# Trunk layer on one core: modulation sums of the first two k-tiles in one PSUM bank, squares of x added in pairs, and a new table for the background sums

## The chip, the cores and the metric

One NeuronCore of a Trainium2 chip runs the whole program. The metric is the device time of one execution in microseconds. Every span and duration below is from the hardware profiler.

## The reference, cut to what matters

One layer over 512 tokens of width 2048. All modulation vectors are columns of one product of a single row, silu(c), with the 2048 x 12288 matrix ada_w. The first normalisation and the modulation make h, and h goes through the input projection w_in:

```python
cond = jax.nn.silu(c)
mod = cond @ ada_w[l] + ada_b[l]
sh_m, sc_m, gt_m, sh_f, sc_f, gt_f = jnp.split(mod[:, None, :], 6, axis=-1)
h = rms_norm(x, mix_pre_g[l]) * (1.0 + sc_m) + sh_m
y = token_mixers(h, w_in[l], ...)
x = x + gt_m * rms_norm(y, mix_post_g[l])
h = rms_norm(x, ffn_pre_g[l]) * (1.0 + sc_f) + sh_f
y = conv_glu_ffn(h, ffn_w_up[l], ffn_conv_w[l], ffn_conv_b[l], ffn_w_down[l])
x = x + gt_f * rms_norm(y, ffn_post_g[l])
```

## The kernel before, in words

**Layout.** x is held transposed as 16 k-tiles of 128 channels x 512 tokens. An fp32 product is made of three matmuls on parts (`mm3`, L379 to L382): L380 is hi x hi of weight and h, L382 the weight's remainder `lo`, L381 the remainder `hl` of h. `split` (L364) makes the weight's parts: ScalarE copies `hi` (L373, L376) and, in the shadow form, a second copy `sh` to PSUM (L372); VectorE subtracts to give `lo` (L374, L377). `make_h` (L486) makes `hh` (L490) and the modulated tile (L491) on ScalarE and `hl` (L493) on VectorE for k-tile 0, on GpSimd for the others; `xn` (L495) multiplies x by the norm in the same way (L497).

**Order of the projection.** The columns of w_in that are taken first run in six steps over k (KSTEPS): four steps of two k-tiles (0, 1), (2, 3), (4, 5), (6, 7), and two of four. In each step five groups of columns (nine in the later steps) are multiplied into PSUM banks, and each result is added to a partial sum in SBUF: in step 0 by a copy on ScalarE (L604, L616), later by an addition on VectorE (L606, L618).

**Modulation columns.** h of a k-tile needs its modulation columns. A set `c` of columns (two k-tiles) is made of eight units and a closing entry (`mod_units`, L518). A unit (`gemv_unit`, L410) loads 256 rows of ada_w (512 KB, L415) into one of five `ada` buffers (NADA) and multiplies them by cond: units alternate between GpSimd (ScalarE scales, L430 and L434; GpSimd adds, L435) and VectorE (one instruction for scale and add, L428 and L432). The closing entry joins the two running sums on VectorE (`join`, L439), sums over partitions on TensorE by matmuls with a column of ones (L446), finishes the columns on VectorE (L450 to L452) and makes h of both k-tiles. For k-tiles 0 and 1 a unit is split in halves of 256 KB (L418), each k-tile's half having its own PSUM bank (`first_half`, L500); there units 1 and 4 go to GpSimd (HV), the others to VectorE, and the column sums are L510, L513 and L514.

**The start.** `x_norm` (L461) squares the 16 tiles of x on ScalarE (L471); of every four squares the first two are added on VectorE (L476), and the three results are summed by fp32 matmuls with a matrix of ones (L477), 12 in all; then come the square root (L478) and the reciprocal (L479).

**What sets the order.** All these loads are issued by SyncE's one queue, in the program's order; an issue waits where its buffer is still in use, and all behind it wait with it. The instructions of each engine are placed by a list scheduler, which goes by costs of its own. In the loop over KSTEPS (L656) closing and other entries of the sets are issued behind the groups: FS0 gives the numbers behind the groups of step 0, and in step s > 0 `upto` takes just the sets that step s + 1 needs, spread over the groups but the last two. This makes 9, 9, 9, 18 and 18 entries in steps 0 to 4.

Of the kernel before, what the change touches and what calls it, by code (L numbers as in the profile page):

```python
# [12 lines left out]
AF = mybir.ActivationFunctionType  # L13
ALU = mybir.AluOpType
# [6 lines left out]
KT = D // P  # L21
# [16 lines left out]
KSTEPS = [(0, 1), (2, 3), (4, 5), (6, 7), (8, 9, 10, 11), (12, 13, 14, 15)]  # L38
# [211 lines left out]
def trunk_kernel(ctx: ExitStack, tc: tile.TileContext, a: dict, out: bass.AP):  # L250
# [30 lines left out]
    def mt(s="m", shape=(P, 512), dt=F32):  # L281
        return cur[0].tile(list(shape), dt, tag="m", name=nm(s))
# [16 lines left out]
    def mx(s="mx"):  # L299
        return pp.tile([P, 512], F32, tag=mtag(), name=nm(s), bufs=2)  # L300
# [110 lines left out]
    def gemv_unit(accs, eng, uidx, i, half=None, bank=None):  # L411
        w = 512 if half is None else 256
        if half is None:
            raw = araw()
            nc.sync.dma_start(out=raw, in_=a["ada"][uidx])  # L415
        else:
            raw = mt("ada")
            nc.sync.dma_start(out=v2(raw), in_=v2(a["ada"][uidx])[:, :, half * 256:(half + 1) * 256])  # L418
        for j in range(2):
            c1 = cond[:, 2 * i + j:2 * i + j + 1]  # L420
            src = raw[:, j * w:(j + 1) * w]
            if eng not in accs:
                if eng is V and bank is not None:
                    accs[eng] = bank[:, :w]
                else:
                    accs[eng] = galloc("ga")[:, :w]
                if eng is V:
                    V.tensor_scalar(accs[eng], src, c1, None, ALU.mult)  # L428
                else:
                    S.activation(accs[eng], src, AF.Copy, scale=c1)  # L430
            elif eng is V:
                V.scalar_tensor_tensor(accs[eng], src, c1, accs[eng], ALU.mult, ALU.add)  # L432
            else:
                S.activation(src, src, AF.Copy, scale=c1)  # L434
                G.tensor_tensor(accs[eng], accs[eng], src, ALU.add)  # L435

    def join(accs):
        if len(accs) == 2:
            V.tensor_tensor(accs[G], accs[G], accs[V], ALU.add)  # L439
        return accs[G]  # L440
# [12 lines left out]
        return ca, cb  # L453


    xT = []
    for kt in range(KT):
        xT.append(hp.tile([P, 512], F32, tag=f"hl{kt}", name=nm("x")))
# [2 lines left out]
    def x_norm():  # L461

        ss = gp.tile([P, 512], F32, name="rB")
        warm = st(1)
        S.activation(warm, tc0[:, 0:1], AF.Square)
        S.activation(warm, warm, AF.Sqrt)
        ps = mx("xss")
        odd = None
        for kt in range(KT):
            sq = mt("sq")  # L470
            S.activation(sq, xT[kt], AF.Square)  # L471
            if kt % 4 == 0:
                odd = sq
                continue
            if kt % 4 == 1:
                V.tensor_tensor(sq, odd, sq, ALU.add)  # L476
            TE.matmul(ps, ones, sq, start=kt == 1, stop=kt == KT - 1)  # L477
        S.activation(ss, ps, AF.Sqrt, bias=epst, scale=1.0 / D)  # L478
        V.reciprocal(ss, ss)  # L479
        return ss  # L480

    rB = x_norm()

    hh, hl = [None] * KT, [None] * KT

# [11 lines left out]
        (G if kt else V).tensor_tensor(h_, xT[kt], rB, ALU.mult)  # L497
        return h_

    def first_half(kt):  # L500

        accs = {}
        bk = mx("ga")
        for i in range(8):
            gemv_unit(accs, (G if i in HV else V), gada[0][i], i, kt, bk)
        h_ = xn(kt)
        ga = join(accs)
        ps = bk[:, 256:258]
        for j in range(2):
            TE.matmul(ps[:, j:j + 1], ga[:, j * P:(j + 1) * P], ones[:, 0:1], start=True, stop=True)  # L510
        ca, cb = (cp.tile([P, 1], F32, name=nm("ca")) for _ in range(2))
        sl = slice(kt, kt + 1)
        V.scalar_tensor_tensor(ca, ps[:, 0:1], bsc1[:, sl], cv("preg")[:, sl], ALU.add, ALU.mult)  # L513
        V.tensor_tensor(cb, ps[:, 1:2], cv("bsh")[:, sl], ALU.add)  # L514
        make_h(kt, ca, cb, h_)
# [104 lines left out]
    early = [g for g in gin if g[3] is not None]  # L620
    late = [g for g in gin if g[3] is None]
    g0, g1 = early[:2]
    first_half(0)
    tiles, fw = [], []
    for g in (g0, g1):
        fw.append(wraw())
# [17 lines left out]

    for i, t, ps in tiles:
        first_mm(i, t, ps, (0,))
    first_half(1)
    for i in range(2):
        first_w(i, 1)
    for i, t, ps in tiles:  # L650
# [2 lines left out]
    ps = acc()  # L653
    first_mm(1, 3, ps, (0, 1))
    ev_early_fm(g1[1][3], ps, 0)
    nextc = 1  # L656
    for s, ks in enumerate(KSTEPS):
        gs = [g for g in early if g[3] == s]
        fs = []
        upto = (KSTEPS[s + 1][-1] + 1) // 2 if s + 1 < len(KSTEPS) else 8  # L660
        while nextc < upto:
            fs += list(mod_units(nextc))
            nextc += 1
        for i, g in enumerate(gs):
            if s == 0 and i < 2:
                pass
            elif g[0] == "FM":
                fm_group(g, ev_early_fm)
            else:
                tm_group(g, ev_early_tm)  # L670
            n = -(-len(fs) // max(1, len(gs) - 2 - i)) if s else FS0[i]
            for f in fs[:n]:
                f()
            fs = fs[n:]

    nc.sync.dma_start(out=cst[:, P:], in_=a["cst"][:, P:])
    mixd = dp.tile([KT, P, 512], F32, name="mixd")
# [159 lines left out]
    for key, base, c_, sl in (("k", 4, 0.5, slice(1, 3)), ("q", 0, 0.5 * QK, slice(0, 4, 3))):  # L837
        ebias = cp.tile([P, 1], F32, name=nm("ebias"))
        G.memset(ebias, EPS / (c_ * c_))
        for h in range(H):  # L840
            y = conv_silu2((key, h), base + h)
            sq = mt("sq")
# [836 lines left out]
RATE = (1, 1, 2, 2, 3, 3, 3)  # L1679
NGA = 3  # L1680
NBR = 5
HV = (1, 4)
FS0 = (1, 4, 4, 3, 3)
NA0 = 2
SH_IN = True

# [15 lines left out]
```

## Time and profile before

| | |
|---|---|
| three runs, us | 2345.55, 2336.04, 2333.36 (median 2336.04) |
| the profiled execution, us | 2339.47 |
| its span, us | 2337.3 |
| its mean granted TensorE clock | 0.978 |
| TensorE busy | 2196.1 us, 94% of the span |
| VectorE, ScalarE, GpSimd busy | 1691.9, 1454.9, 1081.9 us (72%, 62%, 46%) |

The span runs from the first to the last instruction, and 2.2 us of the execution's time lie around it. Busy time counts an instruction as a whole; a matmul's recorded duration (0.40 us) is longer than the distance to the next (0.24 us at full clock), so that distances between starts are used for its cost. In the timeline a number in brackets is the idle time of the engine just before, with what ended it.

### The profile page before, as it was taken

What the parts mean: (1) busy time and instruction counts of PE and PEld (TensorE: products, weight loads), DVE (VectorE), ACT (ScalarE), POOL (GpSimd) and SP (SyncE); (2) the same over time, 40 slices, a digit from 0 to 9 for tenths busy, and PEclk for the clock granted to TensorE, in tenths of its full rate; (3) what the DMA queues carried; (4) which work ended last, traced back from release to release, by engine and by line L of the source; (5) the groups of instructions that cost most, each with busy time, mean ns of one, the idle gap of its engine ahead of it and who ended that gap; (6) DMA issues with size and microseconds to landing.
All of it is one profiled execution on the core that took longest, in us unless ns stands there. A gap on an engine that the chain in (4) does not pass through costs nothing. (4 is left out here: it accounts for less than half of the span.)

```text
span 2337.3 us, 31341 instructions
## 1 busy us (share of the span) xinstructions
PE 2196.1 (94%) x9868; PEld 1738.5 (74%) x9868; DVE 1691.9 (72%) x2659; ACT 1454.9 (62%) x2633; POOL 1081.9 (46%) x847
## 2 busy tenths in 40 slices
PE   5999999989998998899999999999999999999998
PEld 3877876777776786677778887787787777777776
DVE  5877679977878645865655568787787866767777
ACT  5767465354566544566667677776776767666663
POOL 4563022243232200456545465755755665574643
PEclk8999999999999999999999999999999989999999
DMA  8866555677887743778763547455555634425333
GB/s 298 284 249 237 169 180 181 209 237 248 291 307 280 247 140 119 243 263 285 276 213 129 184 169 267 163 193 208 193 186 209 226 109 157 167 100 187 129 127 139
DMA packets 206029, 479.19 MB, mean 205 GB/s; under 512 B 32660, under 2 KB 74148, under 8 KB 205864
## 3 DMA queue, kind: packets, MB, share of 16 engines
q1 hardware_dynamic: 199032, 476.14, 58.5%
q10 hardware_dynamic: 6832, 1.06, 0.3%
q8 instruction: 78, 1.28, 0.2%
q14 instruction: 87, 0.71, 0.1%
HBM read 398.46 MB, written 78.67 MB: 204 GB/s over the span
## 5 line engine op out<-in xcount | busy, mean ns | idle before, releaser
L1494 PE MATMUL X<-hi,ah 128*128 128x512 f32 x960 | 386.2, 403 | 19.1 <-DVE c L1506 11.4
L435 POOL TENSOR_TENSOR ga<-ga,ada 128x512 f32<-128x512 f32 (+1 forms) x167 | 228.5, 1368 | 370.6 <-ACT ada L434 346.7
L1495 PE MATMUL X<-lo,ah 128*128 128x512 f32 x960 | 383.8, 400 | 4.0 <-DVE lo L1457 3.0
L1496 PE MATMUL X<-hi,al 128*128 128x512 f32 x960 | 383.6, 400 | 0.0
L1460 DVE TENSOR_TENSOR lo<-raw,hi 128x512 fp32r<-128x512 f32 x360 | 270.0, 784 | 104.6 <-ACT hi L1459 104.4
L1481 POOL TENSOR_TENSOR raw<-raw 128x512 f32<-128x512 f32 x120 | 161.9, 1353 | 339.6 <-ACT hi L1456 223.2
L1455 ACT ACTIVATE sh<-raw 128x512 fp32r<-128x512 f32 x360 | 210.7, 588 | 141.5 <-DMA raw<-w_dn 65.7
L1494 PE MATMUL Z<-hi,ah 128*128 128x512 f32 x720 | 287.4, 399 | 5.7 <-ACT c L1504 3.2
L1457 DVE TENSOR_TENSOR lo<-raw,sh 128x512 fp32r<-128x512 f32 x360 | 239.7, 683 | 72.2 <-ACT sh L1455 43.1
L1496 PE MATMUL Z<-hi,al 128*128 128x512 f32 x720 | 286.6, 398 | 2.6 <-POOL al L1431 2.6
L1495 PE MATMUL Z<-lo,ah 128*128 128x512 f32 x720 | 286.2, 398 | 0.0
L1459 ACT ACTIVATE hi<-raw 128x512 fp32r<-128x512 f32 x360 | 212.4, 625 | 83.9 <-PE X L1496 30.3
L1456 ACT ACTIVATE hi<-raw 128x512 fp32r<-128x512 f32 x360 | 220.8, 621 | 33.9 <-PE Z L1496 22.3
L1494 PEld LDWEIGHTS X<-hi,ah 128*128 128x128 f32 x960 | 182.7, 190 | 66.9 <-DVE c L1506 9.7
L380 PE MATMUL acc<-hh,hi 128*128 128x512 f32 x544 | 222.4, 412 | 9.5 <-ACT lt L764 7.0
L382 PE MATMUL acc<-hh,lo 128*128 128x512 f32 x544 | 221.3, 410 | 4.6 <-DVE lo L374 4.6
L381 PE MATMUL acc<-hl,hi 128*128 128x512 f32 x544 | 222.8, 410 | 0.5 <-POOL hl L493 0.3
L1495 PEld LDWEIGHTS X<-lo,ah 128*128 128x128 f32 x960 | 183.2, 191 | 46.3 <-DVE lo L1457 3.9
L1496 PEld LDWEIGHTS X<-hi,al 128*128 128x128 f32 x960 | 182.9, 191 | 42.3
L1494 PEld LDWEIGHTS Z<-hi,ah 128*128 128x128 f32 x720 | 136.4, 190 | 41.6 <-ACT c L1504 5.5
L432 DVE SCALAR_TENSOR_TENSOR ga<-ada,cond,ga 128x512 f32<-128x512 f32 (+1 forms) x183 | 151.8, 829 | 17.5 <-DMA ada<-ada 15.3
L377 DVE TENSOR_TENSOR lo<-raw,hi 128x512 fp32r<-128x512 f32 (+1 forms) x162 | 118.9, 748 | 62.8 <-ACT hi L376 61.6
(369 smaller groups left out, 4683.2 us busy)
## 6 DMA issues: line engine op xcount, KB each, us to landing
ada<-ada SPq DMA_DIRECT2D x184, 512.0 KB, 4.5
raw<-w_up SPq DMA_DIRECT2D x172, 512.0 KB, 6.0
raw<-w_dn SPq DMA_DIRECT2D x86, 512.0 KB, 5.7
raw<-w_in SPq DMA_DIRECT2D x56, 512.0 KB, 5.2
partd<-c SPq DMA_DIRECT2D x80, 256.0 KB, 4.4
c<-partd SPq DMA_DIRECT2D x80, 256.0 KB, 4.5
actd<-q SPq DMA_DIRECT2D x40, 512.0 KB, 3.2
ar<-actd SPq DMA_DIRECT2D x35, 512.0 KB, 3.2
```

Source lines behind the costliest of these rows:

```text
L380: TE.matmul(o, sh, mh, start=first, stop=False)
L381: TE.matmul(o, sh, ml, start=False, stop=False)
L382: TE.matmul(o, sl, mh, start=False, stop=last)
L435: G.tensor_tensor(accs[eng], accs[eng], src, ALU.add)
L1455: S.activation(sh, src, AF.Copy)
L1456: S.activation(h_, src, AF.Copy)
L1457: V.tensor_tensor(l_, src, sh, ALU.subtract)
L1459: S.activation(h_, src, AF.Copy)
L1460: eng.tensor_tensor(l_, src, h_, ALU.subtract)
L1494: TE.matmul(ps, ah[:, sl], wh, start=st_, stop=False, skip_group_check=True)
L1495: TE.matmul(ps, ah[:, sl], wl, start=False, stop=False, skip_group_check=True)
L1496: TE.matmul(ps, al[:, sl], wh, start=False, stop=sp_, skip_group_check=True)
```

## The change

**Sums of k-tiles 0 and 1.** `half_sums` runs the eight half units of a k-tile. Both k-tiles use the two halves of one PSUM bank `hbank`, and their column sums go to the first two columns of each half, in the same bank. k-tile 0's are issued ahead of x, k-tile 1's behind `x_norm`. For k-tile 1 all eight units go to VectorE, and a copy to SBUF (L465) takes the place of the join. **Squares** are added in pairs on VectorE: 8 additions and 8 fp32 matmuls instead of 4 and 12. **Table AHEAD** gives the numbers of entries behind each group: 13, 12, 12, 11 and 15 in steps 0 to 4.

```diff
@@ -453,6 +453,19 @@
         return ca, cb
 
 
+    hbank = mx("ga")
+
+    def half_sums(kt):
+
+        accs, bk = {}, hbank[:, kt * 256:(kt + 1) * 256]
+        for i in range(8):
+            gemv_unit(accs, (G if i in HV[kt] else V), gada[0][i], i, kt, bk)
+        if G not in accs:
+            accs[G] = galloc("ga")[:, :256]
+            V.tensor_copy(accs[G], accs.pop(V))
+        return join(accs), bk[:, 0:2]
+
+    half0 = half_sums(0)
     xT = []
     for kt in range(KT):
         xT.append(hp.tile([P, 512], F32, tag=f"hl{kt}", name=nm("x")))
@@ -465,21 +478,18 @@
         S.activation(warm, tc0[:, 0:1], AF.Square)
         S.activation(warm, warm, AF.Sqrt)
         ps = mx("xss")
-        odd = None
-        for kt in range(KT):
-            sq = mt("sq")
-            S.activation(sq, xT[kt], AF.Square)
-            if kt % 4 == 0:
-                odd = sq
-                continue
-            if kt % 4 == 1:
-                V.tensor_tensor(sq, odd, sq, ALU.add)
-            TE.matmul(ps, ones, sq, start=kt == 1, stop=kt == KT - 1)
+        for kt in range(0, KT, 2):
+            s0, s1 = mt("sq"), mt("sq")
+            S.activation(s0, xT[kt], AF.Square)
+            S.activation(s1, xT[kt + 1], AF.Square)
+            V.tensor_tensor(s0, s0, s1, ALU.add)
+            TE.matmul(ps, ones, s0, start=kt == 0, stop=kt == KT - 2)
         S.activation(ss, ps, AF.Sqrt, bias=epst, scale=1.0 / D)
         V.reciprocal(ss, ss)
         return ss
 
     rB = x_norm()
+    half1 = half_sums(1)
 
     hh, hl = [None] * KT, [None] * KT
 
@@ -497,15 +507,10 @@
         (G if kt else V).tensor_tensor(h_, xT[kt], rB, ALU.mult)
         return h_
 
-    def first_half(kt):
-
-        accs = {}
-        bk = mx("ga")
-        for i in range(8):
-            gemv_unit(accs, (G if i in HV else V), gada[0][i], i, kt, bk)
+    def first_half(kt, sums):
+
+        ga, ps = sums
         h_ = xn(kt)
-        ga = join(accs)
-        ps = bk[:, 256:258]
         for j in range(2):
             TE.matmul(ps[:, j:j + 1], ga[:, j * P:(j + 1) * P], ones[:, 0:1], start=True, stop=True)
         ca, cb = (cp.tile([P, 1], F32, name=nm("ca")) for _ in range(2))
@@ -620,7 +625,7 @@
     early = [g for g in gin if g[3] is not None]
     late = [g for g in gin if g[3] is None]
     g0, g1 = early[:2]
-    first_half(0)
+    first_half(0, half0)
     tiles, fw = [], []
     for g in (g0, g1):
         fw.append(wraw())
@@ -644,7 +649,7 @@
 
     for i, t, ps in tiles:
         first_mm(i, t, ps, (0,))
-    first_half(1)
+    first_half(1, half1)
     for i in range(2):
         first_w(i, 1)
     for i, t, ps in tiles:
@@ -653,25 +658,20 @@
     ps = acc()
     first_mm(1, 3, ps, (0, 1))
     ev_early_fm(g1[1][3], ps, 0)
-    nextc = 1
+    fs = [f for c in range(1, 8) for f in mod_units(c)]
     for s, ks in enumerate(KSTEPS):
-        gs = [g for g in early if g[3] == s]
-        fs = []
-        upto = (KSTEPS[s + 1][-1] + 1) // 2 if s + 1 < len(KSTEPS) else 8
-        while nextc < upto:
-            fs += list(mod_units(nextc))
-            nextc += 1
-        for i, g in enumerate(gs):
+        for i, g in enumerate(g for g in early if g[3] == s):
             if s == 0 and i < 2:
                 pass
             elif g[0] == "FM":
                 fm_group(g, ev_early_fm)
             else:
                 tm_group(g, ev_early_tm)
-            n = -(-len(fs) // max(1, len(gs) - 2 - i)) if s else FS0[i]
+            n = AHEAD[s][i] if s < len(AHEAD) else 0
             for f in fs[:n]:
                 f()
             fs = fs[n:]
+    assert not fs
 
     nc.sync.dma_start(out=cst[:, P:], in_=a["cst"][:, P:])
     mixd = dp.tile([KT, P, 512], F32, name="mixd")
@@ -1679,8 +1679,8 @@
 RATE = (1, 1, 2, 2, 3, 3, 3)
 NGA = 3
 NBR = 5
-HV = (1, 4)
-FS0 = (1, 4, 4, 3, 3)
+HV = ((1, 4), ())
+AHEAD = ((1, 4, 4, 2, 2), (3, 3, 2, 2, 2), (3, 3, 2, 2, 2), (3, 3, 3, 1, 1), (3, 3, 3, 2, 2, 1, 1, 0, 0))
 NA0 = 2
 SH_IN = True
 
```

In the changed program the column sums are L515, L518 and L519, the additions of squares L485, their matmuls L486, the reciprocal L488, k-tile 0's `hl` L503, `xn` L507, and L606 and L618 have become L611 and L623; the lines up to L452 are the same.

TensorE at its first matmuls of the projection, before (ga_192 and ga_283 are the sums' banks of k-tiles 0 and 1, hh_238 and hh_329 their h):

```order
L381 MATMUL acc_261<-hl_241,hi_251 128x512
L382 MATMUL acc_261<-hh_238,lo_252 128x512
L510 MATMUL ga_283<-ones,ga_290 128x1 x2
L380 MATMUL acc_255<-hh_329,hi_335 128x512
L380 MATMUL acc_256<-hh_329,hi_335 128x512
L380 MATMUL acc_257<-hh_329,hi_335 128x512
```

and there after the change (ga_103 is the one bank, hh_272 and hl_275 are k-tile 0's):

```order
L486 MATMUL xss_177<-sq_220,ones 128x512
L515 MATMUL ga_103<-ones,ga_110 128x1 x2
L515 MATMUL ga_103<-ones,ga_260 128x1 x2
L380 MATMUL acc_289<-hh_272,hi_280 128x512
L380 MATMUL acc_290<-hh_272,hi_280 128x512
L380 MATMUL acc_291<-hh_272,hi_280 128x512
L380 MATMUL acc_292<-hh_272,hi_280 128x512
```

Both k-tiles' column sums now stand ahead of the first product. VectorE behind the reciprocal, up to k-tile 0's columns, before:

```order
L432 SCALAR_TENSOR_TENSOR ga_192<-ada_217,cond,ga_192 128x256 x2
L432 SCALAR_TENSOR_TENSOR ga_192<-ada_221,cond,ga_192 128x256 x2
L432 SCALAR_TENSOR_TENSOR ga_192<-ada_225,cond,ga_192 128x256 x2
L439 TENSOR_TENSOR ga_199<-ga_199,ga_192 128x256
L513 SCALAR_TENSOR_TENSOR ca_234<-ga_192,bsc_99,colp 128x1
L514 TENSOR_TENSOR ca_235<-ga_192,colp 128x1
L493 TENSOR_TENSOR hl_241<-xn_229,hh_238 128x512
```

and after the change (ada_228 to ada_256 are k-tile 1's units; lo_332 and lo_337 belong to its weights):

```order
L428 TENSOR_SCALAR ga_103<-ada_228,cond 128x256
L507 TENSOR_TENSOR xn_264<-x_141,rB 128x512
L432 SCALAR_TENSOR_TENSOR ga_103<-ada_228,cond,ga_103 128x256
L377 TENSOR_TENSOR lo_332<-raw_277,hi_331 128x512
L432 SCALAR_TENSOR_TENSOR ga_103<-ada_232,cond,ga_103 128x256 x2
L432 SCALAR_TENSOR_TENSOR ga_103<-ada_236,cond,ga_103 128x256 x2
L377 TENSOR_TENSOR lo_337<-raw_278,hi_336 128x512
```

```order
L432 SCALAR_TENSOR_TENSOR ga_103<-ada_252,cond,ga_103 128x256 x2
L432 SCALAR_TENSOR_TENSOR ga_103<-ada_256,cond,ga_103 128x256 x2
L465 COPY ga_260<-ga_103 128x256
L518 SCALAR_TENSOR_TENSOR ca_268<-ga_103,bsc_99,colp 128x1
L519 TENSOR_TENSOR ca_269<-ga_103,colp 128x1
L518 SCALAR_TENSOR_TENSOR ca_321<-ga_103,bsc_99,colp 128x1
```

k-tile 1's 16 instructions of sums and the copy now stand between the reciprocal and k-tile 0's columns (ca_268, ca_269). TensorE in the third group of step 2, before:

```order
L380 MATMUL acc_1017<-hh_780,hi_1005 128x512
L381 MATMUL acc_1017<-hl_783,hi_1005 128x512
L382 MATMUL acc_1017<-hh_780,lo_1006 128x512
L380 MATMUL acc_1017<-hh_787,hi_1011 128x512
L381 MATMUL acc_1017<-hl_790,hi_1011 128x512
L382 MATMUL acc_1017<-hh_787,lo_1012 128x512
```

and the same group after the change (the four tiles acc_1069 to acc_1093):

```order
L380 MATMUL acc_1069<-hh_730,hi_1057 128x512
L381 MATMUL acc_1069<-hl_733,hi_1057 128x512
L380 MATMUL acc_1077<-hh_730,hi_1057 128x512
L381 MATMUL acc_1077<-hl_733,hi_1057 128x512
L380 MATMUL acc_1085<-hh_730,hi_1057 128x512
L381 MATMUL acc_1085<-hl_733,hi_1057 128x512
L380 MATMUL acc_1093<-hh_730,hi_1057 128x512
L381 MATMUL acc_1093<-hl_733,hi_1057 128x512
L382 MATMUL acc_1069<-hh_730,lo_1058 128x512
```

The first k-tile's matmuls without `lo` of all four tiles now stand ahead of the first with `lo`. So it is in groups 3 and 4 of step 2 and groups 2, 3 and 4 of step 3; before it was so in groups 3 and 4 of step 3 alone.

## Rows read from the trace of the kernel before

**Rows 1.** The page, part 1: busy time of each engine and its share of the span.

```profile
PE 2196.1 (94%) x9868; PEld 1738.5 (74%) x9868; DVE 1691.9 (72%) x2659; ACT 1454.9 (62%) x2633; POOL 1081.9 (46%) x847
```

**Rows 2.** Timeline from 0 to 60 us: start, duration, engine, line, out<-in, count, [idle <-releaser].

```profile
6.31 10.18 ACT L471 ACTIVATE sq<-x 128x512 f32<-128x512 f32 x16
...
8.31 13.44 PE L477 MATMUL xss<-sq,ones 128*128 128x512 f32 x24 [8.31 <-DVE sq L476]
...
13.14 11.37 SPq L418 DMA_DIRECT2D ada<-ada  x16
...
21.85 0.69 ACT L478 ACTIVATE rB<-xss,epst 128x512 f32<-128x512 f32 x1 [3.32 <-PE xss L477]
...
22.57 3.35 DVE L479 RECIPROCAL rB<-rB 128x512 f32<-128x512 f32 x1 [2.39 <-ACT rB L478]
```

**Rows 3.** Stretches of the start: length, busy of each engine, granted clock, DMA share, GB/s.

```profile
18.00:20.00 2.00, 2.00 (x6) 0.89 (x5) 1.96 (x4) 0.54 (x1) 0.00 (x0) 1.00 1.09 347
30.00:36.00 6.00, 1.78 (x6) 1.60 (x7) 2.98 (x8) 1.60 (x3) 3.51 (x5) 0.50 1.02 408
```

**Rows 4.** Timeline from 27 us to the end of step 0.

```profile
27.74 4.68 DVE L432 SCALAR_TENSOR_TENSOR ga<-ada,cond,ga 128x256 f32<-128x256 f32 x9
...
32.99 1.01 PE L510 MATMUL ga<-ones,ga 128*128 128x1 f32 x4 [11.24 <-DVE ga L439]
...
35.23 2.07 PE L380 MATMUL acc<-hh,hi 128*128 128x512 f32 x4 [1.22 <-ACT hh L490]
...
40.94 0.63 PE L381 MATMUL acc<-hl,hi 128*128 128x512 f32 x1
...
41.37 0.45 PE L382 MATMUL acc<-hh,lo 128*128 128x512 f32 x1
...
41.65 0.40 PE L380 MATMUL acc<-hh,hi 128*128 128x512 f32 x1
...
41.89 0.39 PE L381 MATMUL acc<-hl,hi 128*128 128x512 f32 x1
...
42.91 1.46 DVE L377 TENSOR_TENSOR lo<-raw,hi 128x512 fp32r<-128x512 f32 x1
...
48.26 2.93 PE L380 MATMUL acc<-hh,hi 128*128 128x512 f32 x6 [1.22 <-ACT hh L490]
...
51.52 0.57 PE L381 MATMUL acc<-hl,hi 128*128 128x512 f32 x1 [0.33 <-POOL hl L493]
...
71.11 0.39 PE L573 MATMUL acc<-hi,hh 128*128 128x264 f32 x1 [0.69 <-ACT pa L604]
```

**Rows 5.** Stretches of steps 1, 2, 3 and 4.

```profile
72.68:99.80 27.12, 26.93 (x131) 21.88 (x130) 23.75 (x41) 23.09 (x42) 20.88 (x17) 1.00 0.81 282
99.80:127.50 27.70, 26.92 (x131) 21.98 (x130) 23.13 (x40) 17.15 (x31) 14.54 (x12) 1.00 0.73 262
127.50:160.10 32.60, 29.70 (x138) 23.68 (x136) 26.86 (x51) 21.84 (x37) 21.94 (x18) 0.95 0.67 251
160.10:215.90 55.80, 53.75 (x260) 44.06 (x259) 41.60 (x71) 38.41 (x68) 26.62 (x21) 1.00 0.74 264
```

**Rows 6.** Groups by line and form from 75 to 200 us: count, busy, mean ns, idle.

```profile
L606 DVE TENSOR_TENSOR pa<-pa,acc 128x512 f32<-128x512 f32 x60 | 40.6, 684 | 8.4 <-PE acc L382 7.1
...
L432 DVE SCALAR_TENSOR_TENSOR ga<-ada,cond,ga 128x512 f32<-128x512 f32 x37 | 27.8, 751 | 1.1 <-DMA ada<-ada 1.0
...
L435 POOL TENSOR_TENSOR ga<-ga,ada 128x512 f32<-128x512 f32 x42 | 54.3, 1293 | 39.2 <-ACT ada L434 35.9 <-POOL ga L435 1.4 <-POOL hl L493 0.4
```

**Rows 7.** Waits of SyncE's queue from 56 to 165 us, and its timeline in step 3.

```profile
SPq L415 <- POOL ga L435: 53.0, 18, 7.7
...
134.34 9.89 SPq L415 DMA_DIRECT2D ada<-ada  x4
```

**Rows 8.** Timeline of step 3's longest stop: ScalarE and TensorE.

```profile
140.38 1.34 ACT L434 ACTIVATE ada<-ada,cond 128x512 f32<-128x512 f32 x2 [2.35 <-DMA ada<-ada]
...
143.50 0.50 PE L382 MATMUL acc<-hh,lo 128*128 128x512 f32 x1 [1.85 <-DVE lo L374]
```

## The prediction, made before the run

> **What bounds the kernel now.** I read the page's busy times first, then the timeline of the start, then stretches and waits of the steps. TensorE is busy 94% of the span [rows 1], so a change can only gain where TensorE stands still or runs at its low clock, and the diff touches two such places. The first is the start, where TensorE has no projection work until 35.23 us [rows 4]. The reader is to see a serial chain there: squares of x end at 6.31 + 10.18 = 16.5 us, their fp32 matmuls at 8.31 + 13.44 = 21.75, square root at 22.5, reciprocal at 25.9 [rows 2]; then VectorE works off k-tile 0's sums, and the column sums begin at 32.99 and the first product at 35.23 [rows 4]. The second is steps 1 to 3. A step has 96 matmuls of 512 columns and 24 of 264. At full clock two starts lie 0.235 us apart (41.65 to 41.89 [rows 4]), and 264/512 of that is 0.12; 96 x 0.235 + 24 x 0.12 + 0.5 for two column sums makes 26.0 us. The steps took 27.12, 27.70 and 32.60 us [rows 5], so they lost 1.1, 1.7 and 6.6, together 9.4. Step 3 has 18 entries of background sums, the others 9, and its longest stop is 1.85 us of waiting for `lo`, behind ScalarE, which had waited 2.35 us for an `ada` load [rows 8]. Step 4, twice as long, lost 55.80 - 52.0 = 3.8.
>
> **The start.** Ahead of x stand now eight loads of 256 KB. They are half of the issues that took 11.37 us [rows 2], so 5.7 us; by bytes 2.1 MB at 347 GB/s [rows 3] take 6.0. I take 6.0: the last square ends at 22.5. One pair addition follows (0.7, as the VectorE addition of that size [rows 6]) and one fp32 matmul (13.44/12 = 1.1). Four matmuls fewer do help: TensorE no longer runs 5 us behind the squares. With 0.1 for the handover the square root begins at 24.4 against 21.85, 2.6 later, and the reciprocal ends at 28.5.
>
> What was meant to be gained, k-tile 0's sums done before x, is lost again by the shared bank. In the new order k-tile 0's column sums stand in that bank, so they come behind the last write of k-tile 1's sums there, the copy. So between the reciprocal and the columns VectorE runs 16 instructions of k-tile 1, x times the norm, two `lo` and the copy: 16 x 0.52 (4.68/9 [rows 4]) + 0.45 + 1.5 for the product and 1.4 for the first `lo`, both beside GpSimd (1.46 [rows 4]), + 0.7 for the second = 12.4. The columns are begun at 40.9 instead of 32.99. From there to the first product it was 35.23 - 32.99 = 2.2, so it starts at 43.2, and 0.2 for the second k-tile's sums makes 43.4: 8.2 later.
>
> Before, though, k-tile 1's products did not begin until 48.26 and ran into a second wait, for its `hl`, until 51.52 [rows 4]. Now both k-tiles' columns are ready together, and the 48 matmuls of both follow without that gap. The clock was at its low level, 0.50 [rows 3], when the products began after the idle stretch, and starts lay 0.43 apart until 41.37 [rows 4], for 6.1 us. The same again takes 14 matmuls to 49.5; the other 34 x 0.235 end at 57.5. Before, six were done by 51.5 and 21 followed: 56.5. So the start costs **+1.0**. Bounds: -1 (neither product nor `lo` slowed by GpSimd, 0.7 us each less, and 5.7 instead of 6.0) to +4 (both `lo` slowed, the low clock for 14 more matmuls at 0.2 each).
>
> k-tile 1's sums on VectorE alone take work from ScalarE and GpSimd (four half instructions each); neither is late there, and I cost this at nothing beyond what VectorE shows above.
>
> **Step 0** gets 13 entries for 9: about two units more for VectorE and two for ScalarE with GpSimd, 2.1 MB of loads. TensorE stands 0.69 us on ScalarE's evictions [rows 4]. I put this at 0, bounds -1 (that wait and some of the sums' cover) to +1.
>
> **Steps 1 to 3** have 12, 12 and 11 entries for 9, 9 and 18. Three entries are 2.7 units, half of them for VectorE. A unit there is two instructions; 0.75 each [rows 6], so 1.5 at most, 1.33 x 1.5 = 2.0 a step, and 0.2 for a third of a join and columns. VectorE's 23.75 and 23.13 [rows 5] become 26.0 and 25.3, in a step of 26.0: **full**. In step 3 seven entries go, 3.1 units for VectorE: 26.86 - 4.7 - 0.5 = 21.7. GpSimd has 1.33 units of two additions at 1.29 [rows 6], 3.4, and a third of the closing entry's four tiles, 1.7: 17.7 on average in steps 1 and 2 becomes 22.8. So the work fits, but VectorE without room, and the new order says the same: the matmuls that need `lo` are put last in half of the groups of steps 2 and 3, which makes a late `lo` cheaper.
>
> A loss in proportion to the entries lies on the line from 1.4 (mean of 9) to 6.6 (18): 3.1, 3.1 and 2.6, 8.8 in all, -0.6. If the steps stayed at 1.4 each it would be 4.2, -5.2. The stops of step 3 look like a queue that overflows (steps 1 and 2 lose little with half the entries), but VectorE is full; I take the middle, 6.4: **-3.0**. Bounds: -9.4 (no loss) to +10.4 (each like step 3, 19.8).
>
> What is moved passes SyncE's queue: 10.7 units of 0.52 MB make 5.6 MB, and the weights are 282 GB/s x 27.12 us [rows 5] less 8 units, 3.5 MB. 9.1 MB at 408 GB/s [rows 3] take 22.3 us of 26.0, which hides them. The Trainium skill, DMA: Bandwidth & Descriptors, section Specifications, puts the limit of one core's HBM traffic at about 358 GB/s. By that the loads take an estimated 25.4 us, with no room left. This kernel's row at 408 speaks against that as a hard limit, and the sum goes by the row.
>
> **Step 4** has 15 entries for 18: 3/18 of its 3.8, **-0.6**, bounds -3.8 to 0. Behind it the order is almost the same, and the gain or loss is carried to the end one to one, since TensorE is the bound there.
>
> **Sum:** +1.0 + 0 - 3.0 - 0.6 = -2.6, on the profiled execution's 2339.47 us 2336.9. That execution lay 3.4 above the median of 2336.04; on the median it is **2333 us**. A measurement of this kernel can tell about 0.5%, 11.7 us.
>
> **Rivals.**
> - **VectorE is the bound of steps 1 and 2**, and what step 3 gains is lost there: the losses stay on the line (-0.6), 1.0 - 0.6 - 0.6 = -0.2, **2336 us**. For it: VectorE at 25 to 26 of 26 us. Against it: its instructions overlap their neighbours by about 0.1 us, so that busy time overstates its need.
> - **The ring of five `ada` buffers closes up in every step (the slower side).** An `ada` load waits for GpSimd's addition, and the weights queued behind it wait along: 53.0 us of such waits in all, up to 7.7 at a time, and four loads issued over 9.9 us in step 3 [rows 7]. ScalarE then waits for `ada` with the copies for `hi` and `sh` behind it [rows 8]. If 12 entries suffice for that in each step, each of the three loses 6.6: +10.4 + 1.0 - 0.6 = +10.8, **2347 us**. It decides once a step's GpSimd work and waits exceed its 26 us. Against it: 22.8 us of need, and steps 1 and 2 lost little with 9.
> - **Everything is smoothed out.** No loss in steps 1 to 4 and the lower bound at the start: -9.4 - 3.8 - 1.0 = -14.2, **2322 us**. For it: the losses stand in the step with 18 entries. Against it: VectorE has no room.
> - That the table does not do what it says can be left out: the entries stand earlier in the new order. That k-tile 0's head start does nothing is part of the forecast.
>
> **How the numbers follow.** Forecast 0.58 (its own range 2328 to 2336, steps 1 to 3 from -5.2 to -0.6, the start within its bounds), full VectorE 0.20, closed ring 0.10, all smoothed 0.12. Eight in ten leaves out most of the two outer cases: 2324 to 2343. Over 0.5% faster (below 2324.4) needs most of the smoothing, half of that case: 0.06. Over 0.5% slower (above 2347.7) is a little less than half of the closed ring: 0.04. The rest, 0.90, is no change that can be told.
>
> **What would show it.** Right: the column sums of both k-tiles begin together near 41 us behind the copy, the first product near 43, its 48 matmuls end near 57.5; steps 1 to 3 take about 28 us each, step 3 four or five less than now; TensorE's waits in steps 1 and 2 are for VectorE. Wrong: k-tile 0's column sums before 36 us; a step 3 that still takes over 31 us; steps 1 or 2 over 30 with ScalarE waiting for `ada`; or a difference of more than 3 us behind step 4, where I count none.

## The result and the profile after

The changed kernel took 2357.67 us (median of 6 runs, 2353.30 to 2362.45), the kernel before beside it 2335.49. The ratio is 1.0089, interval 1.0070 to 1.0107: **22 us slower**. Forecast were 2333 us, 2324 to 2343.

The page of the changed kernel, part 1; the span is 2355.6 us, 18.3 longer:

```profile
PE 2193.0 (93%) x9860; PEld 1734.4 (74%) x9860; DVE 1698.5 (72%) x2667; ACT 1454.5 (62%) x2629; POOL 1081.9 (46%) x844
```

The engines do the work of [rows 1]; TensorE waits longer. The start in its timeline, from the square root to the first product (columns as in [rows 2]):

```profile
25.39 0.69 ACT L487 ACTIVATE rB<-xss,epst 128x512 f32<-128x512 f32 x1 [0.65 <-PE xss L486]
...
26.11 3.35 DVE L488 RECIPROCAL rB<-rB 128x512 f32<-128x512 f32 x1 [0.64 <-ACT rB L487]
...
35.83 5.20 DVE L432 SCALAR_TENSOR_TENSOR ga<-ada,cond,ga 128x256 f32<-128x256 f32 x10
...
41.07 0.42 DVE L465 COPY ga<-ga 128x256 f32<-128x256 f32 x1
...
41.55 1.01 PE L515 MATMUL ga<-ones,ga 128*128 128x1 f32 x4 [16.26 <-DVE ga L465]
...
43.81 2.48 PE L380 MATMUL acc<-hh,hi 128*128 128x512 f32 x5
```

Against [rows 4] the column sums come at 41.55 instead of 32.99, behind the copy L465, and the first product at 43.81 instead of 35.23. Both were forecast, at 40.9 and 43.4. The stretches of steps 1 to 4 (columns as in [rows 5]):

```profile
74.71:101.44 26.73, 26.56 (x131) 21.83 (x130) 24.45 (x40) 21.95 (x40) 21.79 (x17) 1.00 0.69 249
101.44:131.26 29.82, 28.02 (x138) 22.75 (x137) 24.19 (x44) 17.47 (x30) 15.80 (x13) 1.00 0.72 255
131.26:172.44 41.18, 31.19 (x130) 24.65 (x130) 28.92 (x51) 25.39 (x43) 24.18 (x19) 0.85 0.70 253
172.44:225.74 53.30, 53.30 (x258) 44.33 (x258) 39.04 (x68) 36.48 (x63) 20.74 (x16) 0.99 0.75 251
```

Step 1 starts 2.0 us later than before. Steps 1 and 4 are shorter than in [rows 5], step 2 is 2.1 longer, and **step 3, with 11 entries instead of 18, takes 41.18 us instead of 32.60**. By the end of step 4 the changed kernel is 9.9 us behind. In its longest stop SyncE (SPq is its queue of loads), ScalarE, GpSimd, VectorE and TensorE stand behind each other (rows of each engine's own timeline, by time):

```profile
115.78 10.75 SPq L415 DMA_DIRECT2D ada<-ada  x3
126.62 0.38 SPq L351 DMA_DIRECT2D raw<-w_in  x1
127.10 5.84 SPq L415 DMA_DIRECT2D ada<-ada  x3
...
128.60 1.34 ACT L434 ACTIVATE ada<-ada,cond 128x512 f32<-128x512 f32 x2 [4.76 <-DMA ada<-ada]
...
129.46 2.65 POOL L435 TENSOR_TENSOR ga<-ga,ada 128x512 f32<-128x512 f32 x2 [3.29 <-ACT ada L434]
...
133.66 0.63 ACT L373 ACTIVATE hi<-raw 128x512 fp32r<-128x512 f32 x1 [2.71 <-DMA raw<-w_in]
...
139.06 0.72 ACT L434 ACTIVATE ada<-ada,cond 128x512 f32<-128x512 f32 x1 [2.85 <-DMA ada<-ada]
139.69 0.58 ACT L372 ACTIVATE sh<-raw 128x512 fp32r<-128x512 f32 x1
...
140.30 0.69 DVE L374 TENSOR_TENSOR lo<-raw,sh 128x512 fp32r<-128x512 f32 x1 [7.35 <-ACT sh L372]
...
141.05 0.80 PE L382 MATMUL acc<-hh,lo 128*128 128x512 f32 x1 [7.66 <-DVE lo L374]
```

It goes round twice. Three loads of `ada` are issued over 10.75 us, the last two of them at 124.95 and 126.20, since each waits for its buffer. ScalarE waits 4.76 us for one of these, and GpSimd's additions, which free the buffers, start behind it at 129.46. So the next two loads (the end of the row at 127.10) are issued only at 132.14 and 132.52, and ScalarE waits 2.85 us again, now with the copy `sh` behind it. A weight's load, issued at 126.62 behind the three, costs ScalarE another 2.71 us on the way. VectorE waits 7.35 us for `sh`, TensorE 7.66 for `lo`. It is the stop of [rows 8], four times as long.

The other 8.4 us come later. To find them I compared starts: for each instruction of ScalarE, VectorE and SyncE's queue with the same name and as many instances in both traces, its start in the one less its start in the other, and the median over a stretch. The changed kernel is 9.9 behind at 230 to 260 us, 4.6 at 1300 to 1410, then 11.7 at 1470 to 1540, 12.4 at 1780 to 1830, and 20.0 at 1930 to 1960. So it loses **7 near 1425 us and 8 near 1870 us**, in the FFN, which the diff does not touch. The 5 that it gains ahead of 1410 are not explained; two traces of the same order differ by about 3 there (below, rotation late).

### The profile page after: what moved, and what is told of

The parts are those of the page before. It is cut to its first block, busy times and chain, and to the rows that moved or that the text cites. A ratio compares the mean times of both kernels' runs of the same rounds, so it can differ in the third digit from the quotient of the medians.

```text
span 2355.6 us, 31322 instructions
## 1 busy us (share of the span) xinstructions
PE 2193.0 (93%) x9860; PEld 1734.4 (74%) x9860; DVE 1698.5 (72%) x2667; ACT 1454.5 (62%) x2629; POOL 1081.9 (46%) x844
## 5 line engine op out<-in xcount | busy, mean ns | idle before, releaser
L1459 ACT ACTIVATE hi<-raw 128x512 fp32r<-128x512 f32 x360 | 211.7, 624 | 82.1 <-PE Z L1496 26.4
L1456 ACT ACTIVATE hi<-raw 128x512 fp32r<-128x512 f32 x360 | 220.4, 621 | 34.4 <-PE Z L1496 23.1
L1494 PEld LDWEIGHTS X<-hi,ah 128*128 128x128 f32 x960 | 182.0, 190 | 65.7 <-DVE c L1506 10.2
```

What stands on the lines that cost most here:

```text
L1456: S.activation(h_, src, AF.Copy)
L1459: S.activation(h_, src, AF.Copy)
L1494: TE.matmul(ps, ah[:, sl], wh, start=st_, stop=False, skip_group_check=True)
```

## The experiments

What the change does there is seen in its code and order. Later PSUM tiles and the copies `sh` take their tag from a counter that alternates between two tags (`mtag`, `mx`). With one bank for two k-tiles the counter is called once less, so **every later tile whose tag comes from the counter lies in the other tag**. The order of TensorE then differs from before, beyond the projection's steps, at just two places, those near 1425 and 1870 us. The theory (A): the table costs 8 to 10 us through the loop of `ada` buffers, the turned rotation the rest. The rivals: the rotation costs it all, or the late places are chance.

Times of each run follow with their ratio to runs of the kernel before beside them. "Step" columns are from one profile each, from a step's first 512-column matmul to the next step's.

| run | us (median) | ratio, interval | step 1 starts | steps 1, 2, 3, 4 |
|---|---|---|---|---|
| before | 2335.49 | | 72.7 | 27.1, 27.7, 32.7, 55.6 |
| changed | 2357.67 | 1.0089 (1.0070 to 1.0107) | 74.7 | 26.7, 29.8, 41.2, 53.3 |
| rotation alone | 2350.78 | 1.0055 (1.0033 to 1.0076) | 71.2 | 26.5, 27.0, 33.5, 54.0 |
| changed, rotation undone | 2349.18 | 1.0053 (1.0033 to 1.0072) | 79.5 | 26.8, 31.3, 37.6, 54.4 |
| table alone | 2344.77 | 1.0032 (1.0019 to 1.0045) | 73.3 | 26.8, 28.8, 40.9, 53.0 |
| changed, two banks | 2336.87 | 1.0005 (0.9989 to 1.0020) | 67.4 | 27.3, 31.5, 33.7, 53.9 |
| start alone | 2339.03 | 1.0008 (0.9993 to 1.0024) | 74.1 | 26.6, 28.1, 33.8, 53.8 |
| two banks, old table | 2335.05 | 0.9987 (0.9972 to 1.0002) | 68.2 | 26.4, 26.4, 37.6, 53.9 |
| table, no scaling | 2335.85 | 0.9995 (0.9977 to 1.0014) | 72.0 | 27.3, 27.4, 30.9, 55.3 |
| table, no addition | 2334.52 | 0.9998 (0.9979 to 1.0016) | 71.0 | 26.8, 28.0, 30.9, 53.0 |
| rotation late | 2350.31 | 1.0059 (1.0038 to 1.0080) | 72.0 | 27.4, 26.6, 34.4, 53.5 |
| two banks, third table | 2333.66 | 0.9989 (0.9976 to 1.0003) | 69.9 | 27.3, 28.3, 34.0, 53.1 |
| squares alone | 2336.50 | 0.9992 (0.9973 to 1.0010) | 70.6 | 26.8, 26.9, 33.3, 53.9 |
| rotation back late | 2346.77 | 1.0051 (1.0030 to 1.0072) | 74.3 | 26.8, 29.8, 39.5, 52.9 |

### The rotation

**Rotation alone:**

```diff
     nextc = 1
+    mtag()
     for s, ks in enumerate(KSTEPS):
```

> The kernel before with one more turn of the rotation of PSUM tags ahead of the loop over k, and nothing else: every later tile of the rotating tags lies in the other of the two tags. Theory A (the table makes the loop of ada buffers stall in steps 2 and 3, and the turned rotation costs only what it changes near 1425 and 1870 us): steps 1 to 4 as before within 1 us (27, 28, 33, 56), 5 to 10 us lost behind 1400 us, 2341 to 2346 us. Theory B (the turned rotation makes all of the loss): step 3 about 41 us, 2354 us or more. Theory C (the two steps behind 1400 us are chance): 2336 us.

It took 2350.78 us, 13 more than the kernel before beside it, where theory A had 5 to 10, with steps 1 to 4 about as before (2.2 us less in all). Its profiled execution, at 2339.88 us, is far below its median; even there the starts fall back by 5.5 us between 1410 and 1470 and by 3.8 between 1830 and 1930.

**Rotation late**, to see whether it costs behind the mixing part alone:

```diff
         mixing_open[0] = False
+        mtag()
```

> The kernel before with one more turn of the tag rotation where the FFN begins (near 920 us): all of the mixing part is as before, and the two places near 1425 and 1870 us have the order that they have with the turn at the start. Theory A (the loss by the turned rotation lies at these two places): 2345 to 2352 us, with jumps of 5 to 7 us near 1425 and 3 to 8 near 1870 in the comparison of starts, and nothing ahead of 920 us. Rival (the turn costs in the mixing part): 2336 to 2341 us.

2350.31 us, 14 more; by 1410 it is 3.2 us ahead of the kernel before, with the same order up to there, then it loses 6.1 and 7.5 at the two places. So the turned rotation, put alone into the kernel before, costs 13 to 14 us, and the FFN is where. Windows at the two places, before, changed and late (columns as in [rows 3], the first lines of each answer left out):

```profile
1400.00:1460.00 60.00, 59.35 (x254) 47.39 (x254) 52.10 (x71) 46.05 (x83) 35.63 (x24) 1.00 0.74 259
1860.00:1920.00 60.00, 51.82 (x217) 40.68 (x216) 42.23 (x57) 39.58 (x70) 33.83 (x31) 0.89 0.46 166
```

```profile
1400.00:1460.00 60.00, 55.12 (x222) 43.18 (x221) 39.78 (x53) 42.74 (x75) 41.54 (x27) 0.94 0.57 211
1860.00:1920.00 60.00, 48.46 (x198) 37.51 (x197) 39.68 (x48) 33.18 (x57) 35.63 (x30) 0.83 0.42 151
```

```profile
1400.00:1460.00 60.00, 55.10 (x226) 43.16 (x226) 43.16 (x62) 41.75 (x74) 34.05 (x21) 0.97 0.71 248
1860.00:1920.00 60.00, 48.96 (x199) 37.57 (x198) 39.08 (x51) 34.78 (x61) 28.17 (x25) 0.86 0.45 162
```

In 60 us TensorE starts 28 to 32 matmuls less near 1425, and in the second stretch 18 or 19 less. The order of ScalarE at the first place, before and then with the rotation turned late:

```
L1459 ACTIVATE hi_13024<-raw_12702 128x512
L1455 ACTIVATE sh_13180<-raw_13160 128x512
L1459 ACTIVATE hi_13034<-raw_12706 128x512
L1455 ACTIVATE sh_13195<-raw_13164 128x512
L1459 ACTIVATE hi_13044<-raw_12710 128x512
L1504 ACTIVATE c_12964<-Z_12914 128x512
```

```
L1460 ACTIVATE hi_13024<-raw_12702 128x512
L1460 ACTIVATE hi_13034<-raw_12706 128x512
L1460 ACTIVATE hi_13044<-raw_12710 128x512
L1505 ACTIVATE c_12964<-Z_12914 128x512
L1431 ACTIVATE ah_12968<-ar_12970 128x1024
L1505 ACTIVATE c_12966<-Z_12915 128x512
```

Before, the copies sh_13180 and sh_13195 of the next weights stand early; turned, they stand behind all of this and more. In the traces, the kernel before first, TensorE then ScalarE:

```profile
1426.55 0.39 PE L705 MATMUL gtps<-gh,ones_r 128*128 128x512 f32 x1
```

```profile
1410.09 0.59 ACT L1455 ACTIVATE sh<-raw 128x512 fp32r<-128x512 f32 x1
...
1411.13 0.59 ACT L1455 ACTIVATE sh<-raw 128x512 fp32r<-128x512 f32 x1
```

and with the rotation turned late (lines of this kernel are one higher than before's):

```profile
1423.32 0.39 PE L705 MATMUL gtps<-gh,ones_r 128*128 128x512 f32 x1
...
1427.53 0.51 PE L1495 MATMUL Z<-hi,ah 128*128 128x512 f32 x1 [2.65 <-ACT c L1505]
1428.90 0.79 PE L1496 MATMUL X<-lo,ah 128*128 128x512 f32 x1 [0.86 <-DVE lo L1458]
```

```profile
1426.90 0.58 ACT L1505 ACTIVATE c<-X 128x512 f32<-128x512 f32 x1
1427.38 1.11 ACT L1456 ACTIVATE sh<-raw 128x512 fp32r<-128x512 f32 x2
```

The first two `sh` stood 16 and 15 us ahead of the matmul into `gtps`; turned, they come 4.1 us behind it, so `lo` is late. TensorE takes Z's matmul with `hi` in the meantime, which waits for an eviction, and then runs at the low clock: its starts lie 0.43 us apart up to 1432.05, at a granted clock of 0.50.

```profile
1429.00:1432.00 3.00, 3.00 (x7) 2.38 (x8) 0.49 (x2) 1.49 (x4) 2.92 (x3) 0.50 1.04 395
```

Why at these two places: where all tiles follow the counter, turning it renames them all alike. Here one side has its tag fixed in the code. The copies `sh` of the first place always take `mxb` (L1479), while `gtps` follows the counter (L704); the tiles `cT` of the second always take `mxa` (L1577), while the copies `sh` of the next weights follow it. In the built programs `gtps` lies in PSUM bank 2 before and the `sh` in banks 0 and 1; with the rotation turned late `gtps` lies in bank 0, in the changed kernel in bank 1, among them. At the second place the first `sh` moves from bank 1 into those of `cT` (2 and 3). So the tiles share a tag in the turned kernels only. That this is what made the scheduler put the copies later is inferred from it; no run changed those two tags.

**Changed, rotation undone** and **changed, rotation back late**: one call of `mtag()` behind the first two k-tiles, or one where the FFN begins (as in the diff above).

```diff
     fs = [f for c in range(1, 8) for f in mod_units(c)]
+    mtag()
```

> The changed kernel with one more turn of the rotation behind the first two k-tiles, so that all later tiles lie in the tags of before. Theory A: step 3 stays near 41 us, +10 by 220 us, but nothing more is lost near 1425 and 1870 us: 2343 to 2347 us. Theory B: step 3 as in the forecast, 28 us, about 2333 us. Theory C: like the changed kernel, 2350 us or more.

> The changed kernel with the rotation of tags turned back where the FFN begins (near 920 us): the mixing part is that of the change, the two places near 1425 and 1870 us have the order of before. Theory A (the table and the start cost about 8 to 10 us by the end of step 4, the turned rotation about 13 behind 1400 us): step 3 near 40 us as in the change, no jump at the two places, 2343 to 2348 us. Rival (the costs do not add up): the time of the change, 2354 us or more.

They took 2349.18 and 2346.77 us, by their ratios 8 to 9 us less than the changed kernel. With the rotation back late step 3 is still 39.5 us, and the starts move by -0.3 and -0.2 us at the two places; with it undone, by 0.1 and -1.0. The first is not a clean removal: the turn so early also changes TensorE's order in steps 0 to 3, step 1 starts 4.8 us later than in the changed kernel, and theory A's figures (2343 to 2347) were too low. The second has the changed kernel's order up to the FFN and that of before at the two places, and lies within its 2343 to 2348.

### The table

**Table alone**, the new loop and AHEAD in the kernel before:

```diff
+    fs = [f for c in range(1, 8) for f in mod_units(c)]
...
-        upto = (KSTEPS[s + 1][-1] + 1) // 2 if s + 1 < len(KSTEPS) else 8
...
-            n = -(-len(fs) // max(1, len(gs) - 2 - i)) if s else FS0[i]
+            n = AHEAD[s][i] if s < len(AHEAD) else 0
```

> The kernel before with the new table alone (13, 12, 12, 11, 15 entries). Theory A: step 3 about 40 us, steps 1 to 4 together 9 to 12 us longer than before, 2344 to 2348 us. Theory B: step 3 about 28 us, 2330 to 2333 us.

2344.77 us, 7 more (0.32%), as theory A had it, though steps 1 to 4 together are 6.3 us longer and not 9 to 12. Steps 2 and 3 take 69.7 us against 60.4, with the same kind of stop in step 3, without any change at the start:

```profile
137.84 0.80 PE L382 MATMUL acc<-hh,lo 128*128 128x512 f32 x1 [6.85 <-DVE lo L374]
```

**Table, no scaling** and **table, no addition** break the loop at two links (the table's own lines are left out here; the test is false for units of sets 1 to 7):

```diff
-                S.activation(src, src, AF.Copy, scale=c1)
+                if half is not None or not early_on[0]:
+                    S.activation(src, src, AF.Copy, scale=c1)
                 G.tensor_tensor(accs[eng], accs[eng], src, ALU.add)
```

> The new table alone, with ScalarE's scaling (L434) left out in the units of sets 1 to 7 that go to GpSimd: these units are added without their factor. ScalarE then has no instruction that waits for a load of ada rows ahead of the copies sh and hi, but the loads, GpSimd's additions and the ring of five buffers stay. Theory A1 (the copies sh stand behind a scaling that waits for its load, in ScalarE's order): steps 2 and 3 together near 54 us instead of 70. Theory A2 (SyncE's queue stands for a free buffer, and weights come late): both steps stay over 60 us together.

```diff
                 S.activation(src, src, AF.Copy, scale=c1)
-                G.tensor_tensor(accs[eng], accs[eng], src, ALU.add)
+                if half is not None or not early_on[0]:
+                    G.tensor_tensor(accs[eng], accs[eng], src, ALU.add)
```

> The new table alone, with GpSimd's addition (L435) left out in the units of sets 1 to 7: only the first of each set's GpSimd terms is kept. A buffer is then free when ScalarE has scaled it, up to 2.6 us and a wait earlier, while the scalings stand in ScalarE's order as before. Theory A2 (the loads wait for GpSimd's release): SyncE's waits for GpSimd go, and steps 2 and 3 take together 54 to 58 us. Theory A1 with loads that are slow by themselves: over 62 us.

Steps 2 and 3 of the table alone, without the scaling, and without the addition:

```profile
100.05:128.88 28.83, 28.36 (x139) 22.65 (x137) 26.45 (x46) 17.44 (x30) 16.69 (x13) 1.00 0.75 273
128.88:169.73 40.85, 31.28 (x131) 24.79 (x130) 28.28 (x48) 25.26 (x43) 23.30 (x18) 0.87 0.71 241
```

```profile
99.30:126.68 27.38, 27.38 (x138) 22.80 (x137) 24.70 (x46) 13.42 (x23) 18.14 (x16) 1.00 0.84 304
126.68:157.56 30.88, 27.99 (x131) 21.97 (x130) 29.01 (x48) 16.29 (x28) 17.95 (x14) 1.00 0.68 242
```

```profile
97.84:125.86 28.02, 27.79 (x139) 22.89 (x137) 25.22 (x45) 18.66 (x32) 5.16 (x4) 1.00 0.83 303
125.86:156.80 30.94, 28.84 (x130) 23.37 (x130) 27.25 (x47) 22.35 (x39) 9.16 (x7) 0.94 0.75 257
```

Either cut takes 11 us off: 58.3 and 59.0 instead of 69.7, and the whole time is that of the kernel before again. Both missed their figures a little (54, and 54 to 58). SyncE's queue waits for GpSimd, in the table alone and without the scaling, by the lists of waits from 56 to 225 us (us in total, times, longest):

```profile
SPq L415 <- POOL ga L435: 62.9, 23, 7.0
```

```profile
SPq L416 <- POOL ga L437: 64.1, 26, 5.0
```

So the buffers' slow release alone does not stop TensorE as before (theory A2 by itself falls, narrowly: 58.3 us against its 60 and more); it does so when ScalarE's scaling, which waits for the late load, stands ahead of `sh` (A1). Without the addition the release is early, and ScalarE's waits for `ada` in steps 2 and 3, with scalings still ahead of the copies, fall from 17.0 to 6.3 us:

```profile
ACT ada L434 <- DMA ada<-ada: 17.0, 7, 4.0
```

```profile
ACT ada L435 <- DMA ada<-ada: 6.3, 5, 2.2
```

ScalarE's work as such is not the reason, since it is 41.0 us of 59.0 there and was 42.7 of 69.7. Cutting either link removes the long stop; but the scheduler placed ScalarE's instructions of these steps anew in both runs, so that neither cut changes its link alone. VectorE, at 29.01 of 30.88 us, is full in step 3 in the run without scaling, and there TensorE loses 5 us only.

**Two banks, third table** (13, 12, 9, 11 and 18 entries) asked whether fewer entries in step 2 are enough; its two banks are explained under The start:

```diff
-AHEAD = ((1, 4, 4, 2, 2), (3, 3, 2, 2, 2), (3, 3, 2, 2, 2), (3, 3, 3, 1, 1), (3, 3, 3, 2, 2, 1, 1, 0, 0))
+AHEAD = ((1, 4, 4, 2, 2), (3, 3, 2, 2, 2), (3, 3, 3, 0, 0), (4, 4, 3, 0, 0), (3, 3, 3, 3, 2, 2, 2, 0, 0))
```

> Two banks for the sums, and a table of 13, 12, 9, 11 and 18 entries: steps 0 and 1 run ahead as in the change, steps 2 and 3 are relieved in the way that the change had in mind for step 3 alone, step 4 is as before. If the stops grow with the entries of a step: steps 1 to 3 27, 27 and 30 us, 2329 to 2332 us. Rival (any table that runs ahead lets the scheduler put scalings that wait for a load ahead of the copies sh, whatever the count): step 3 over 34 us, 2336 us or more.

2333.66 us, between the two: step 2 takes 28.3 us, step 3 34.0, with a stop of 3.69 us for `lo`. The count of entries in step 3 does not foretell its length: 11 entries gave from 33.7 to 41.2 us in the runs with all links, 18 from 32.7 to 37.6.

### The start

**Start alone**, the changed kernel with the old table and rotation:

```diff
-    fs = [f for c in range(1, 8) for f in mod_units(c)]
...
+    mtag()
...
+        upto = (KSTEPS[s + 1][-1] + 1) // 2 if s + 1 < len(KSTEPS) else 8
...
-            n = AHEAD[s][i] if s < len(AHEAD) else 0
+            n = -(-len(fs) // max(1, len(gs) - 2 - i)) if s else FS0[i]
```

> The changed kernel with the old table (9, 9, 9, 18, 18 entries) and the old rotation of tags: only the shared bank with k-tile 0's sums ahead of x, and the pairs of squares, are left. If the costs add up (the rotation +13, the table +7, together the +20 of the change), this is about +4 by the difference of the run with the rotation undone and the one with the table alone: 2339 to 2343 us. Theory A, start as forecast (+1.0): step 0 ends 1 to 3 us later than before, step 3 near 33 us. Rival (the shared bank delays the whole loop, and the table is innocent with it): step 3 over 37 us.

2339.03 us, +0.08%, within its error of nothing; step 1 starts 1.4 us late. **Changed, two banks**, and **two banks, old table**, which has the loop of the last diff without `mtag()` besides:

```diff
-    hbank = mx("ga")
...
-        accs, bk = {}, hbank[:, kt * 256:(kt + 1) * 256]
+        accs, bk = {}, mx("ga")
...
-        return join(accs), bk[:, 0:2]
+        return join(accs), bk[:, 256:258]
```

> The changed kernel with a PSUM bank for each of the two k-tiles' sums, which also keeps the rotation of before. The column sums of k-tile 0 no longer wait for k-tile 1's copy: the first product starts near 32 us instead of 43.8; k-tile 1's columns still come near 41, so that TensorE stands again between the two and step 0 ends at most 3 us earlier. Theory A: step 3 still about 40 us, 2340 to 2346 us. Theory B: 2328 to 2333 us.

> The changed kernel with two banks for the sums and the old table: the head start and the pairs of squares without the shared bank, the turned rotation and the new table. Theory A: step 1 starts near 67 us as it did with two banks, 5 us earlier than before, and steps 2 and 3 take 28 and 33 us; 2330 to 2333 us, the fastest so far. Rival (the head start only moves the wait into the loop): 2336 to 2338 us.

TensorE with two banks and the new table:

```profile
31.67 2.08 PE L380 MATMUL acc<-hh,hi 128*128 128x512 f32 x4 [6.96 <-ACT hh L499]
```

The first product starts at 31.67 instead of 43.81 and step 1 at 67.4 instead of 74.7: the shared bank cost the head start, 7 us. With the new table the whole comes out even with before, with the old one 0.13% under it, neither clear of the error. Both theories missed the first: step 3 is 33.7 us, neither 40 nor 28. A bank each is its only edit against the changed kernel, and it takes the ratio from 1.0089 to 1.0005: **the shared bank, with the turn of the tags that comes with it, carries nearly all of the loss**, and the table's cost is not seen where the head start is kept. With the old table step 1 starts 4.5 us earlier than before; step 3 takes 4.9 back (37.6 us, a stop of 4.46 for `lo`), the other steps are shorter, and 3.3 us are left at the end of step 4. The median is 3.5 us under the kernel before beside it, between theory A and the rival. **Squares alone**, the pairs in the kernel before:

```diff
...
-            if kt % 4 == 1:
-                V.tensor_tensor(sq, odd, sq, ALU.add)
-            TE.matmul(ps, ones, sq, start=kt == 1, stop=kt == KT - 1)
...
+            V.tensor_tensor(s0, s0, s1, ALU.add)
+            TE.matmul(ps, ones, s0, start=kt == 0, stop=kt == KT - 2)
```

> The kernel before with the squares added in pairs alone. The square root starts about 3.5 us earlier (18.4 instead of 21.85) since TensorE has 8 fp32 matmuls instead of 12 and no longer runs behind the squares. If VectorE's chain from the reciprocal sets the first product, it starts about 3 us earlier, and step 1 1 to 3 us earlier: 2336 us. Rival (the loads of the second half set step 0): nothing by the start of step 1.

0.08% less, within the error. In its profile step 1 starts 2.1 us earlier, but the column sums come at 31.40 against 32.99, 1.6 earlier and not 3; three kernels whose start is untouched (rotation alone, rotation late, table alone) began step 1 between 71.2 and 73.3, so most of that may be chance.

## Why the prediction was wrong, point by point

- **"Behind it the order is almost the same, and the gain or loss is carried to the end one to one": this step failed, and cost most.** Two swaps of a few matmuls in the order were priced at nothing. The rotation that makes them costs 13 to 14 us put alone into the kernel before; undone in the changed kernel it gives back 8 to 9 of the 22. No rival held it, but the signs of being wrong did: over 3 us behind step 4, where 8.4 came.
- **Steps 1 to 3, forecast -3.0, measured +10.2** (26.7 + 29.8 + 41.2 against 27.1 + 27.7 + 32.7). The mechanism was in the prediction as the slower rival, with 0.10 and a price of +10.4, each of three steps losing 6.6. It closed in steps 2 and 3 alone, 3.8 and 15.2 over 26.0; step 1 lost 0.7. That the total agrees with the rival's price to 0.2 us is luck, since no step lost its 6.6. The measured time lies over that rival's 2347 too, by the rotation. The choice of the middle was wrong. What was taken for it, that 12 entries overflow less than 18, is what failed: the loss is not set by the count. The argument that GpSimd's need (22.8 of 26 us) leaves room was no reason either, since no engine was full in step 3; a chain of waits through SyncE, ScalarE and GpSimd made the stop.
- **"VectorE is the bound of steps 1 and 2"**: it is not. VectorE was busy 24.45 us of 26.73 in step 1 and 24.19 of 29.82 in step 2, against 26.0 and 25.3 forecast; TensorE's longest stop, in step 3, was VectorE's wait for ScalarE's `sh`.
- **The start, forecast +1.0, with step 0 0:** +2.0, inside the bounds. The square root came at 25.39 (24.4), the copy ended at 41.5 (40.9), the first product at 43.81 (43.4): the loads ahead of x cost 1 us more than the 2.6 counted, VectorE's chain 0.4 less than its 12.4. That the shared bank undoes the head start was right, and two banks show its size, 7 us by step 1.
- **Step 4, forecast -0.6:** -2.3, inside the bounds.
- **The page of the Trainium skill** (DMA: Bandwidth & Descriptors, Specifications, about 358 GB/s for a core's HBM): steps 2 and 3 moved 255 and 253 GB/s, against 262 and 251 before [rows 5], so the mean rate shows no limit that made the loss. Between 123 and 126 us, at 14 GB/s, the loads all but stood still while SyncE waited for a buffer. The row at 408 [rows 3] speaks against it as a hard limit for this core running alone.

Put one by one into the kernel before, the parts come to the whole within the error: rotation 0.55 to 0.59%, table 0.32%, start 0.08%, together 0.95 to 0.99%, against 0.89% (0.70 to 1.07). Taken out of the changed kernel the rotation is worth less, 0.36 to 0.38%; each interval is about 0.2% to either side, so how the 22 us divide is not known more closely than that.

## What to carry to other kernels

An edit that allocates one rotating PSUM tile more or less moves every later tile of the rotation to another tag, and so against the tiles whose tag is fixed; where a scheduler sets the order, compare the order to the end of the program, and price even a swap of six matmuls by the waits at that place, or keep the number of allocations. A background load is not paid by its share of engine time: ask which engine has an instruction that waits for it, and what stands behind in that engine's order. And a head start is worth nothing when its result lies in a bank that another sum writes later.

## What was not expected

- At one place where copies of 0.58 us stand later in ScalarE's order, TensorE did 28 to 32 matmuls less in 60 us.
- Leaving ScalarE's scaling out took steps 2 and 3 from 69.7 to 58.3 us, though ScalarE was busy only 42.7 of the 69.7.
- The kernel before itself ranged from 2326.23 to 2352.80 us over the runs beside these experiments, about 1.1%, so that only sets of 6 to 12 runs told differences of 0.3%.
